# Differential-attention scores as one matmul per component instead of two, with a higher scheduling priority for the softmax chain

## The chip, the cores and the metric

The kernel runs on one core of one Trainium2 chip. The metric is the device time of one execution, in microseconds (us). Before the change it is 1974.8 us, the median of three runs (1973.25 to 1975.01). The engines are named as the profile names them: PE (TensorE, the matmul engine; PEld is its weight load), DVE (VectorE), ACT (ScalarE), POOL (GpSimd) and SP (the queue that issues the transfers). PEclk is the granted TensorE clock; 1.00 is 2.4 GHz.

## The reference, cut to what matters

Two decoder layers work on 512 tokens of 1024 features. Each layer is a feed-forward part, a mixer of four parallel groups, and a second feed-forward part. The change touches one group of the mixer, the differential attention: four heads of 64 features, each cut into two components of 32, causal, in four blocks of 128 queries.

```python
def _differential_attention(q, k, v, lam, lam_init, out_g):
    def one_block(args):
        qi, i = args
        s = jnp.einsum('bqhcd,bkhcd->bhcqk', qi, k).astype(jnp.float32) * scale
...
        p = jax.nn.softmax(jnp.where(causal, s, NEG_INF), axis=-1)
        a = p[:, :, 0] - lam * p[:, :, 1]
        return jnp.einsum('bhqk,bkhe->bqhe', a.astype(v.dtype), v)
```

So a head has two score matrices (c = 0 and 1), two softmaxes, and one product of their weighted difference with v. The queries and keys are RMS-normalised first.

## The kernel before

Every dense product is computed in a reduced-precision matmul type three times, to come close to float32: both factors are split into a high part and a low remainder, and `mm3` (L336 to L339) issues high by high, high by low and low by high. The weights are split on the chip, chunk by chunk in four pieces: ACT casts the high part (`wh`, L288) and DVE subtracts it (`wl`, L289). A ring of three buffers holds the raw chunks and their two halves.

The mixer projects its groups one after another: the convolution (`b`), queries and keys of the differential attention (`aqk`), its values (`av`), queries and keys of the second attention (`dqk`), its values and gates (`dvf`), the gating group (`c`), then the output projection (`wo`). When the columns of a group are there, a Python generator is started for its chain (`chain_a` for the differential attention), and every `mm3` call advances a clock by the matmul time that it stands for; when a chain's next step is due, its instructions are written between the matmuls of the projection that is running. So the attention runs in the shadow of `dqk`, `dvf` and `c`, and these matmuls are what PE does while a softmax is on DVE and ACT. The scheduler then orders each engine's queue by priority, which is the order of writing unless a block is wrapped in `tc.high_priority(offset=HX)`, which counts its instructions as written HX places earlier. Each engine works through its queue in order.

`attention_gen` (L1037) runs 16 units per layer, one for each head and query block, block fastest. Its step s multiplies the weights of unit s-2 with v (`weigh_v`, tile `poA`, then ACT scales into `oa`, L1035), computes scores and softmax of unit s (`stage1_a`, L1173), and transposes the weights of unit s-1 on PE (`ptA`, L1021) with a copy from PSUM by ACT (`pT`, L1026).

In `stage1_a` each component has a score tile `scA` of 128 queries by (i+1)*128 keys: two matmuls (high keys `aTh`, remainder of the keys `aTs`) and one matmul that adds the mask. `softmax` (L1004) takes the negated row maximum on DVE (`nmA`, L1007) and the exponential with its row sum on ACT (`p`, L1009). DVE then computes the reciprocal of both sums (`rA`, L1182), the factor `cf` (L1184) and the merged weights (`p`, L1185). The four blocks are 128, 256, 384 and 512 keys wide.

`prep_a` (L1200) makes the operands of one head, once for the queries (w = 0) and once for the keys (w = 1). The normalised columns `zr` hold each component twice (components 0, 0, 1, 1 in 32 columns each); PE transposes them to 128 rows (`aT`). For the queries ACT writes a scaled high part `aTh` (L1207) and, per component, a scaled copy masked by `gA` (`aTx`, L1212), and DVE combines the two with a `slot` pattern (`aTs`, L1214): in the 64 rows of the component lie the high part and the remainder, in the other 64 rows zeros. For the keys ACT writes the high part and DVE the remainder, both over all 128 rows (L1219). Head 0 is prepared at the start of the chain, each further head inside the units of the head before it (blocks 1 and 2).

Of the kernel before, what the change touches and what calls it, by code (L numbers as in the profile page):

```python
# [9 lines left out]
F32 = mybir.dt.float32  # L10
F32R = mybir.dt.float32r
BF16 = mybir.dt.bfloat16
I32 = mybir.dt.int32
AF = mybir.ActivationFunctionType
# [3 lines left out]
P = 128  # L18
# [6 lines left out]
def tile_hybrid_trunk(  # L25
# [47 lines left out]
    RSA, RSO, RSD, RSC, RSG = 0, 0, 0, 1, 1  # L73
    HX = 20
    Q = D // 4
# [16 lines left out]
    def blk(dt=F32, name="blk"):  # L92
        return bpool.tile([P, 512], dt, tag="blk", name=name)
# [68 lines left out]


    slot = const.tile([P, 2, 2], F32, name="slot")
    V.memset(slot, 0.0)
    for r in range(4):
        V.memset(slot[32 * r : 32 * r + 32, r // 2, 0:1], 1.0 - 2.0 * (r % 2))
        V.memset(slot[32 * r : 32 * r + 32, r // 2, 1:2], float(r % 2))
    fold = const.tile([P, P], F32, name="fold")
# [851 lines left out]
    def transpose_p(p, i, name):  # L1021
        pt = att(f"pt{name}")
        for j in range(i + 1):
            transpose(out=pt[:, j * P : (j + 1) * P], in_=p[:, j * P : (j + 1) * P], identity=ident)
        pT = blk(name="pT")
        A.copy(pT[:, : (i + 1) * P], pt[:, : (i + 1) * P])  # L1026
        return pT
# [43 lines left out]
    def mixer(l, hn, before, nxt):  # L1071
# [16 lines left out]
        V.tensor_scalar(ogs, cols[:, col_at["og"] + l : col_at["og"] + l + 1], 1.0 - lam_init, None, ALU.mult)  # L1088
        gA = small.tile([P, 4], F32, tag="gA", name=f"gA{l}")
        a0 = col_at["aq"] + 2 * l  # L1090
        V.tensor_scalar(gA[:, 0:1], cols[:, a0 : a0 + 1], 32 ** -0.5, None, ALU.mult)
        V.tensor_copy(gA[:, 1:2], cols[:, a0 + 1 : a0 + 2])
        V.tensor_scalar(gA[:, 2:4], slot[:, :, 1], gA[:, 0:1], None, ALU.mult)
        gD = small.tile([P, 2], F32, tag="gD", name=f"gD{l}")
# [78 lines left out]
        def stage1_a(i, hd):  # L1173
# [4 lines left out]
            for cc in range(2):  # L1178
                q, (kh, kl) = aT[hd][0][cc], aT[hd][1]
                sc = scores(((q, kh), (q, kl)), i, f"A{l}{i}{hd}{cc}", False)  # L1180
                pp.append(softmax(sc, n, s[:, cc : cc + 1], f"A{l}{i}{hd}{cc}"))
            V.reciprocal(r, s)  # L1182
            cf = small.tile([P, 1], F32, tag="cf", name=f"cf{l}{i}{hd}", bufs=4)
            V.scalar_tensor_tensor(cf, s[:, 0:1], nlam, r[:, 1:2], ALU.mult, ALU.mult)  # L1184
            V.scalar_tensor_tensor(pp[0][:, :n], pp[1][:, :n], cf, pp[0][:, :n], ALU.mult, ALU.add)  # L1185
            if hd < H - 1 and i in (1, 2):
# [13 lines left out]
        def prep_a(hd, w):  # L1200


            ps = att(f"aT{l}{hd}{w}")
            for t in range(NT):
                transpose(out=ps[:, t * P : (t + 1) * P], in_=zr[t, w][:, hd * P : (hd + 1) * P], identity=ident)
            hi = blk(F32R, "aTh")
            A.activation(hi, ps, AF.Identity, scale=gA[:, w : w + 1])  # L1207
            if w == 0:
                sts = []
                for cc in range(2):  # L1210
                    x_low = blk(name="aTx")
                    A.activation(x_low, ps, AF.Identity, scale=gA[:, 2 + cc : 3 + cc])  # L1212
                    st = blk(F32R, "aTs")
                    V.scalar_tensor_tensor(st, hi.bitcast(F32), slot[:, cc, 0:1], x_low, ALU.mult, ALU.add)  # L1214
                    sts.append(st)
                aT[hd] = [sts]
            else:
                st = blk(F32R, "aTs")
                V.scalar_tensor_tensor(st, ps, gA[:, 1:2], hi.bitcast(F32), ALU.mult, ALU.subtract)  # L1219
                aT[hd].append((hi, st))  # L1220

# [237 lines left out]
```

## Time and profile before

| | before |
|---|---|
| median of three runs | 1974.8 us |
| the profiled execution | 1977.86 us |
| its span in the trace | 1976.1 us (1.8 us lie around it) |
| PE busy | 1954.2 us, 99% |
| DVE busy | 1226.9 us, 62% |
| ACT busy | 725.1 us, 37% |
| granted TensorE clock, mean | 0.993 |

The busy shares are means over the whole span. The differential attention runs from about 454 us to 550 us in the first layer and about 970 us later in the second, so stretches of 10 us are read there. In a timeline a row is one instruction or a run of equal ones: start, time from the first start to the last end, engine, line, operation, output and inputs. Matmuls overlap, and the distance from one start to the next is what a matmul costs PE; the duration printed is longer. The bracket at a row's end is idle time of the engine just before it and the instruction that ended it.

### The profile page before, as it was taken

The numbers are of one execution on the slowest core, as the hardware profiler recorded it, in microseconds if no ns is written. First come the engines' busy times: TensorE is split into PE (matmuls) and PEld (weight loads), VectorE is DVE, ScalarE is ACT, GpSimd is POOL, SyncE is SP. The second block draws the span as 40 slices with busy tenths as digits, with TensorE's granted clock in tenths as the row PEclk, the third lists the DMA queues.
The fourth block names the chain that finished last, engine by engine and source line by source line (L and its number), as shares of the span: only waits on it lengthen the run. The fifth ranks groups of instructions, "written<-read, shape, count | busy, mean of one in ns | idle before, by whom it ended". The sixth has DMA issues, their size and how long they took to land.

```text
span 1976.1 us, 26140 instructions
## 1 busy us (share of the span) xinstructions
PE 1954.2 (99%) x10264; PEld 1661.3 (84%) x10264; DVE 1226.9 (62%) x2608; ACT 725.1 (37%) x1512; POOL 5.6 (0%) x18
## 2 busy tenths in 40 slices
PE   9999999999999999999999999999999999999999
PEld 7888888997889888888898888889887898888888
DVE  6776675588977776677575334337987773333332
ACT  4423222345764322323242222233366643222230
POOL 0000000000000000000000000000000000000000
PEclk8999999999999999999999999999999999999999
DMA  9665655221212566465433332322212122322311
GB/s 299 198 234 195 213 210 192 82 74 65 70 44 66 178 206 230 179 228 193 148 126 131 107 106 86 107 86 92 70 59 70 43 78 82 119 101 92 106 64 43
DMA packets 165350, 250.54 MB, mean 127 GB/s; under 512 B 6292, under 2 KB 112236, under 8 KB 165228
## 3 DMA queue, kind: packets, MB, share of 16 engines
q1 hardware_dynamic: 164640, 247.73, 37.2%
q8 instruction: 80, 1.31, 0.3%
q0 software_dynamic: 352, 1.05, 0.2%
q14 instruction: 42, 0.34, 0.1%
q10 hardware_dynamic: 236, 0.10, 0.0%
HBM read 246.76 MB, written 2.10 MB: 126 GB/s over the span
## 4 chain that ended last, share of the span: by engine, by line
PE 92%; DVE 5%; issue 1%; DMA 1%; ACT 1%; SPq 0%
PE i L337 15%; PE i L338 15%; PE i L339 15%; PE o L337 8%; PE o L338 8%; PE o L339 8%; PE wo L337 1%; DVE cacc L1130 1%; PE wo L339 1%; PE wo L338 1%; PE scA L143 1%; PE scD L143 1%; DVE wl L289 1%; PE poD L143 1%; PE dqk L337 1%
## 5 line engine op out<-in xcount | busy, mean ns | idle before, releaser
L289 DVE TENSOR_TENSOR wl<-w,wh 128x512 fp32r<-128x512 f32 (+3 forms) x652 | 401.2, 663 | 319.9 <-ACT wh L288 319.4
L288 ACT CAST wh<-w 128x512 fp32r<-128x512 f32 (+3 forms) x652 | 352.3, 600 | 666.1 <-issue 384.9
L337 PE MATMUL i<-hnh,wh 128*128 128x512 f32 (+1 forms) x1408 | 526.5, 376 | 2.2 <-ACT hnh L630 2.2
L338 PE MATMUL i<-hnl,wh 128*128 128x512 f32 (+1 forms) x1408 | 527.1, 375 | 0.3
L339 PE MATMUL i<-hnh,wl 128*128 128x512 f32 (+1 forms) x1408 | 526.4, 375 | 0.0
L337 PEld LDWEIGHTS i<-hnh,wh 128*128 128x128 f32 x1408 | 264.1, 188 | 49.4 <-ACT hnh L630 2.6
L338 PEld LDWEIGHTS i<-hnl,wh 128*128 128x128 f32 x1408 | 264.9, 188 | 48.0 <-DVE hnl L623 0.7
L339 PEld LDWEIGHTS i<-hnh,wl 128*128 128x128 f32 x1408 | 264.7, 188 | 47.8
L337 PE MATMUL o<-acth,wh 128*128 128x512 f32 (+1 forms) x832 | 297.9, 358 | 0.0
L338 PE MATMUL o<-actl,wh 128*128 128x512 f32 (+1 forms) x832 | 296.8, 357 | 0.0
L339 PE MATMUL o<-acth,wl 128*128 128x512 f32 (+1 forms) x832 | 296.6, 356 | 0.0
L337 PEld LDWEIGHTS o<-acth,wh 128*128 128x128 f32 x832 | 157.2, 189 | 22.6 <-DVE h L868 0.3
L339 PEld LDWEIGHTS o<-acth,wl 128*128 128x128 f32 x832 | 157.2, 189 | 22.6
L338 PEld LDWEIGHTS o<-actl,wh 128*128 128x128 f32 x832 | 157.2, 189 | 22.5
L501 DVE SCALAR_TENSOR_TENSOR acc<-ada,cond,acc 128x512 f32<-128x512 f32 x224 | 154.5, 744 | 24.2 <-DMA ada<-in_ada_w_dram 23.8
L937 DVE TENSOR_TENSOR silu<-silu,i 128x512 f32<-128x512 f32 x82 | 56.3, 687 | 158.5 <-PE i L339 158.5
L939 ACT CAST acth<-silu 128x512 fp32r<-128x512 f32 x88 | 54.4, 618 | 222.6 <-DVE silu L937 222.6
L868 DVE SCALAR_TENSOR_TENSOR h<-o,modc,h 128x512 f32<-128x512 f32 (+1 forms) x112 | 73.9, 671 | 70.6 <-PE o L339 70.0
L1130 DVE SCALAR_TENSOR_TENSOR cacc<-yp,cwc,cacc 128x512 f32<-128x512 f32 x120 | 89.5, 746 | 1.4
L941 DVE TENSOR_TENSOR actl<-silu,acth 128x512 fp32r<-128x512 f32 x88 | 60.5, 688 | 27.5 <-ACT acth L939 27.5
L630 ACT ACTIVATE hnh<-hn,modc 128x256 fp32r<-128x256 f32 x80 | 38.8, 506 | 72.3 <-DVE hn L629 72.3
L934 ACT ACTIVATE silu<-i 128x512 f32<-128x512 f32 x82 | 48.8, 596 | 31.9 <-PE i L339 31.9
(335 smaller groups left out, 2362.5 us busy)
## 6 DMA issues: line engine op xcount, KB each, us to landing
w<-in_ffn_w_in_dram SPq DMA_DIRECT2D x166, 512.0 KB
ada<-in_ada_w_dram SPq DMA_DIRECT2D x64, 1024.0 KB
w<-in_ffn_w_out_dram SPq DMA_DIRECT2D x40, 1024.0 KB
w<-in_w_in_dram SPq DMA_DIRECT2D x18, 1024.0 KB
w<-in_w_out_dram SPq DMA_DIRECT2D x8, 1024.0 KB
w<-in_ffn_w_in_dram SPq DMA_DIRECT2D x18, 256.0 KB
fpb<-in_ada_w_dram SPq DMA_DIRECT2D x16, 256.0 KB
w<-in_ffn_w_out_dram SPq DMA_DIRECT2D x8, 512.0 KB
```

The costliest lines, as they stand in the source:

```text
L143: return T.matmul(out, **kw)
L288: A.copy(wh[:, a], r[:, a])
L289: V.tensor_tensor(wl[:, a], r[:, a], wh[:, a].bitcast(F32), ALU.subtract)
L337: T.matmul(ps, lhsT=lh, rhs=rh, start=start, stop=False)
L338: T.matmul(ps, lhsT=lh, rhs=rl, start=False, stop=False)
L339: last_t[0] = T.matmul(ps, lhsT=ll, rhs=rh, start=False, stop=stop)
L501: last_v[0] = V.scalar_tensor_tensor(acc, src, cond[:, k : k + 1], acc, ALU.mult, ALU.add)
L868: V.scalar_tensor_tensor(h[m][:, a:b], ps[:, a:b], mcol(l, j, m), h[m][:, a:b], ALU.mult, ALU.add)
L937: last_v[0] = V.tensor_tensor(s, s, ps, ALU.mult)
L939: A.copy(ah, s)
L941: V.tensor_tensor(al, s, ah.bitcast(F32), ALU.subtract)
L1130: V.scalar_tensor_tensor(acc, ysl, w, acc, ALU.mult, ALU.add)
```

## The change

The keys get the same layout as the queries had in part: per component `st[cc]` holds 64 rows of the component's own high part and, in the other 64 rows, the remainder. The queries' `st[cc]` holds high part and remainder in the component's own 64 rows, and a copy of them in the other 64. One matmul over 128 rows then gives the sum that two matmuls gave. In `prep_a` the 128-row instructions of DVE become pairs over 64 rows, ACT's second `aTx` falls away, and two copies (queries) and one more activation (keys) of 64 rows come in. HX goes from 20 to 200, and the reciprocal, `cf`, the merge and the copy `pT` are put under it as well; the second attention shares `softmax` and `transpose_p`.

```diff
-    HX = 20
+    HX = 200
...
     def transpose_p(p, i, name):
...
         pT = blk(name="pT")
-        A.copy(pT[:, : (i + 1) * P], pt[:, : (i + 1) * P])
+        with tc.high_priority(offset=HX):
+            A.copy(pT[:, : (i + 1) * P], pt[:, : (i + 1) * P])
         return pT
...
             for cc in range(2):
-                q, (kh, kl) = aT[hd][0][cc], aT[hd][1]
-                sc = scores(((q, kh), (q, kl)), i, f"A{l}{i}{hd}{cc}", False)
+                sc = scores(((aT[hd][0][cc], aT[hd][1][cc]),), i, f"A{l}{i}{hd}{cc}", False)
                 pp.append(softmax(sc, n, s[:, cc : cc + 1], f"A{l}{i}{hd}{cc}"))
-            V.reciprocal(r, s)
             cf = small.tile([P, 1], F32, tag="cf", name=f"cf{l}{i}{hd}", bufs=4)
-            V.scalar_tensor_tensor(cf, s[:, 0:1], nlam, r[:, 1:2], ALU.mult, ALU.mult)
-            V.scalar_tensor_tensor(pp[0][:, :n], pp[1][:, :n], cf, pp[0][:, :n], ALU.mult, ALU.add)
+            with tc.high_priority(offset=HX):
+                V.reciprocal(r, s)
+                V.scalar_tensor_tensor(cf, s[:, 0:1], nlam, r[:, 1:2], ALU.mult, ALU.mult)
+                V.scalar_tensor_tensor(pp[0][:, :n], pp[1][:, :n], cf, pp[0][:, :n], ALU.mult, ALU.add)
...
-            hi = blk(F32R, "aTh")
-            A.activation(hi, ps, AF.Identity, scale=gA[:, w : w + 1])
+            own = (slice(0, 64), slice(64, 128))
+            st = [blk(F32R, "aTs") for _ in range(2)]
             if w == 0:
-                sts = []
+                hi = blk(F32R, "aTh")
+                A.activation(hi, ps, AF.Identity, scale=gA[:, 0:1])
+                x_low = blk(name="aTx")
+                A.activation(x_low, ps, AF.Identity, scale=gA[:, 2:3])
                 for cc in range(2):
-                    x_low = blk(name="aTx")
-                    A.activation(x_low, ps, AF.Identity, scale=gA[:, 2 + cc : 3 + cc])
-                    st = blk(F32R, "aTs")
-                    V.scalar_tensor_tensor(st, hi.bitcast(F32), slot[:, cc, 0:1], x_low, ALU.mult, ALU.add)
-                    sts.append(st)
-                aT[hd] = [sts]
+                    a, b = own[cc], own[1 - cc]
+                    V.scalar_tensor_tensor(st[cc][a], hi[a].bitcast(F32), slot[a, 0:1], x_low[a], ALU.mult, ALU.add)
+                    A.copy(st[cc][b], st[cc][a].bitcast(F32))
+                aT[hd] = [st]
             else:
-                st = blk(F32R, "aTs")
-                V.scalar_tensor_tensor(st, ps, gA[:, 1:2], hi.bitcast(F32), ALU.mult, ALU.subtract)
-                aT[hd].append((hi, st))
+                for cc in range(2):
+                    a, b = own[cc], own[1 - cc]
+                    A.activation(st[cc][a], ps[a], AF.Identity, scale=gA[a, 1:2])
+                    V.scalar_tensor_tensor(st[cc][b], ps[a], gA[a, 1:2], st[cc][a].bitcast(F32), ALU.mult, ALU.subtract)
+                aT[hd].append(st)
```

The queues of SP and POOL keep their order; those of PE, DVE and ACT change between the start of the differential attention and the first matmuls of the output projection. The places below are in the first layer, in the third head (head 2), from its third to its fourth block; the second layer has the same pattern.

PE before, from the second score tile of head 2, block 3 (512 keys): `ptA` x3 transposes the weights of block 2, `poA` x3 multiplies them with v, `dvf` is the projection that runs.

```order
L143 MATMUL scA_4584<-aTh,aTs 128x512
L143 MATMUL scA_4584<-aTs 128x512
L143 LDWEIGHTS identb
L143 MATMUL scA_4584<-maskb,identb 128x128
L339 MATMUL dvf_3_4396<-wh_4153,hnl 128x260
L337 MATMUL dvf_3_4396<-wh_4153,hnh 128x260
L338 MATMUL dvf_3_4396<-wl_4154,hnh 128x260
L339 MATMUL dvf_3_4396<-wh_4153,hnl 128x260
L147 MATMUL ptA_4596<-ident,p 128x128 x3
L337 MATMUL dvf_3_4396<-wh_4153,hnh 128x260
L338 MATMUL dvf_3_4396<-wl_4154,hnh 128x260
```

PE now, from the transposes of block 1 (`ptA` x2) on:

```order
L147 MATMUL ptA_4524<-ident,p 128x128 x2
L143 MATMUL poA_4555<-va,pT 128x64 x2
L143 MATMUL scA_4561<-aTs 128x512
L143 LDWEIGHTS identb
L143 MATMUL scA_4561<-maskb,identb 128x128
L143 MATMUL scA_4568<-aTs 128x512
L143 LDWEIGHTS identb
L143 MATMUL scA_4568<-maskb,identb 128x128
L147 MATMUL ptA_4579<-ident,p 128x128 x3
L143 MATMUL poA_4623<-va,pT 128x64 x3
L143 MATMUL scA_4630<-aTs 128x128
```

No projection matmul stands any more between `ptA` x2 and the transposes of block 3 (`ptA` x4). Before, 22 `dvf` matmuls stood between `ptA` x2 and `poA` x2, four between the scores of block 3 and `ptA` x3, and three between `ptA` x3 and `poA` x3; now all of them come earlier. Behind `ptA` x4 there were six matmuls of `c` ahead of `poA` x4, and now there are four.

ACT before, from the exponentials of block 2 (`p` of 384) to the copy `pT` of block 2, where `aTh` belongs to the preparation of head 3:

```order
L1009 ACTIVATE p,sA_4508<-scA_4510,nmA_4514 128x384
L1009 ACTIVATE p,sA_4508<-scA_4518,nmA_4522 128x384
L1207 ACTIVATE aTh<-aT_4530,gA_3265 128x512
L1026 COPY pT<-ptA_4539 128x256
L1035 ACTIVATE oa<-poA_4570,rA_4436 128x64
L1009 ACTIVATE p,sA_4574<-scA_4576,nmA_4580 128x512
L1009 ACTIVATE p,sA_4574<-scA_4584,nmA_4588 128x512
L1026 COPY pT<-ptA_4596 128x384
```

ACT now, the same stretch, with `wh` of the first chunk of `wo`:

```order
L286 CAST wh_4729<-w_4599 128x512
L1007 ACTIVATE p,sA_4493<-scA_4495,nmA_4498 128x384
L1007 ACTIVATE p,sA_4493<-scA_4502,nmA_4505 128x384
L1220 ACTIVATE aTs<-aT_4513,gA_3264 64x512
L286 CAST wh_4729<-w_4599 128x512 x3
L1220 ACTIVATE aTs<-aT_4513,gA_3264 64x512
L1025 COPY pT<-ptA_4524 128x256
L1034 ACTIVATE oa<-poA_4555,rA_4423 128x64
L1007 ACTIVATE p,sA_4559<-scA_4561,nmA_4564 128x512
L1007 ACTIVATE p,sA_4559<-scA_4568,nmA_4571 128x512
L1025 COPY pT<-ptA_4579 128x384
```

Between the second exponential of block 2 and the copy `pT` of block 1 stood one activation; now three casts and two activations stand there. In the queue before, these casts came behind the copy of block 2.

DVE before, from the row maxima of block 2 to those of block 3 (`dqk` is the normalisation for the second attention, `aTs` the preparation of head 3):

```order
L1007 TENSOR_REDUCE nmA_4522<-scA_4518 128x1
L1279 TENSOR_TENSOR dqk_4426<-zqk,ry_d_4413 128x8x64
L1279 TENSOR_TENSOR dqk_4480<-zqk,ry_d_4413 128x8x64
L1279 TENSOR_TENSOR dqk_4493<-zqk,ry_d_4413 128x8x64
L1182 RECIPROCAL rA_4509<-sA_4508 128x2
L1219 SCALAR_TENSOR_TENSOR aTs<-aT_4530,gA_3265,aTh 128x512
L1184 SCALAR_TENSOR_TENSOR cf_4527<-sA_4508,nlam_3260,rA_4509 128x1
L1279 TENSOR_TENSOR dqk_4544<-zqk,ry_d_4413 128x8x64
L1185 SCALAR_TENSOR_TENSOR p<-p,cf_4527 128x384
L1007 TENSOR_REDUCE nmA_4580<-scA_4576 128x1
```

DVE now, from the merge of block 2 to the row maxima of block 3:

```order
L1184 SCALAR_TENSOR_TENSOR p<-p,cf_4509 128x384
L190 TENSOR_TENSOR rt_d_4401<-ry_d_4400 128x32
L287 TENSOR_TENSOR wl_4590<-w_4394,wh_4589 128x512
L191 SCALAR_TENSOR_TENSOR rt_d_4401<-rt_d_4401,rv_d_4399 128x32
L1221 SCALAR_TENSOR_TENSOR aTs<-aT_4513,gA_3264,aTs 64x512
L192 SCALAR_TENSOR_TENSOR ry_d_4400<-rt_d_4401,ry_d_4400 128x32
L1129 SCALAR_TENSOR_TENSOR cacc<-yp_3566,cwc,cacc 128x512
L1005 TENSOR_REDUCE nmA_4564<-scA_4561 128x1
```

Between the merge of block 2 and the row maxima of block 3 nothing stood before; now a `wl`, the second `aTs` of head 3, a step of the convolution (`cacc`) and three short ones do. Ahead of that merge, behind its row maxima, stand now three `wl`, one `aTs` and six short ones instead of four `dqk`, one `aTs` and two short ones, and all four `dqk` stand between the row maxima and the merge of block 3, where three `wl` and one `cacc` stood.

## Rows read from the trace of the kernel before

**Rows 1.** The page, part 1: busy us, share of span, instructions.

```profile
PE 1954.2 (99%) x10264; PEld 1661.3 (84%) x10264; DVE 1226.9 (62%) x2608; ACT 725.1 (37%) x1512; POOL 5.6 (0%) x18
```

**Rows 2.** Stretches: PE, PEld, DVE, ACT, POOL busy, PEclk, DMA share, GB/s.

```profile
450.00:460.00 10.00, 6.73 (x30) 4.60 (x30) 10.00 (x24) 4.33 (x11) 0.00 (x0) 0.79 0.00 0
...
510.00:520.00 10.00, 8.43 (x62) 7.14 (x61) 10.00 (x25) 7.44 (x24) 0.75 (x1) 1.00 0.29 104
...
1480.00:1490.00 10.00, 8.43 (x62) 7.16 (x60) 10.00 (x25) 7.44 (x23) 0.75 (x1) 1.00 0.30 91
```

**Rows 3.** PE timeline: the second matmul of a score tile, 512 and 128 keys.

```profile
491.99 0.40 PE L143 MATMUL scA<-aTs 128*128 128x512 f32 x1
492.23 0.23 PE L143 MATMUL scA<-maskb,identb 128*128 128x128 bf16 x1
...
496.05 0.28 PE L143 MATMUL scA<-aTs 128*128 128x128 f32 x1
496.16 0.23 PE L143 MATMUL scA<-maskb,identb 128*128 128x128 bf16 x1
```

**Rows 4.** PE timeline: head 2, blocks 1 to 3 (transposes, products with v).

```profile
509.15 0.38 PE L147 MATMUL ptA<-ident,p 128*128 128x128 f32 x2
509.28 0.37 PE L338 MATMUL dvf<-wl,hnh 128*128 128x260 f32 x1
...
512.00 0.55 PE L143 MATMUL poA<-va,pT 128*128 128x64 f32 x4
...
515.84 0.88 PE L143 MATMUL poA<-va,pT 128*128 128x64 f32 x6 [0.89 <-ACT pT L1026]
...
518.00 0.63 PE L147 MATMUL ptA<-ident,p 128*128 128x128 f32 x4 [0.68 <-DVE p L1185]
518.39 0.49 PE L337 MATMUL c<-wh,hnh 128*128 128x512 f32 x1
...
519.87 1.09 PE L143 MATMUL poA<-va,pT 128*128 128x64 f32 x8
```

**Rows 5.** ACT, by line and form: an activation over 66 rows, all 16.

```profile
L1312 ACT ACTIVATE dT<-dT,gD x16: 665/681/690, 534.7 to 1512.1; 66x512 f32<-66x512 f32 x16
```

**Rows 6.** ACT timeline, head 2, blocks 1 to 3.

```profile
509.02 0.58 ACT L1009 ACTIVATE p<-scA,nmA 128x384 f32<-128x384 f32 x1 [0.25 <-DVE nmA L1007]
...
510.16 0.68 ACT L1207 ACTIVATE aTh<-aT,gA 128x512 fp32r<-128x512 f32 x1
510.73 0.37 ACT L1026 COPY pT<-ptA 128x256 f32<-128x256 f32 x1
...
513.97 0.69 ACT L1009 ACTIVATE p<-scA,nmA 128x512 f32<-128x512 f32 x1 [1.08 <-DVE nmA L1007]
...
516.97 1.65 ACT L288 CAST wh<-w 128x512 fp32r<-128x512 f32 x3
```

**Rows 7.** DVE timeline, head 2, blocks 2 and 3.

```profile
509.47 1.89 DVE L1279 TENSOR_TENSOR dqk<-zqk,ry_d 128x512 f32<-128x512 f32 x3
...
511.35 0.73 DVE L1219 SCALAR_TENSOR_TENSOR aTs<-aT,gA,aTh 128x512 fp32r<-128x512 f32 x1
...
512.73 0.61 DVE L1185 SCALAR_TENSOR_TENSOR p<-p,cf 128x384 f32<-128x384 f32 x1
513.25 1.28 DVE L1007 TENSOR_REDUCE nmA<-scA 128x1 f32<-128x512 f32 x2
514.45 1.29 DVE L289 TENSOR_TENSOR wl<-w,wh 128x512 fp32r<-128x512 f32 x2
...
516.45 0.74 DVE L1130 SCALAR_TENSOR_TENSOR cacc<-yp,cwc,cacc 128x512 f32<-128x512 f32 x1
```

**Rows 8.** PE timeline: the idle stretch of 452 us and the matmuls behind it.

```profile
454.20 0.33 PE L147 MATMUL aT<-ident,zr 128*128 128x128 f32 x1 [2.06 <-DVE zr L1227]
...
457.94 0.77 PE L337 MATMUL dqk<-wh,hnh 128*128 128x512 f32 x1
...
462.56 0.40 PE L338 MATMUL dqk<-wl,hnh 128*128 128x512 f32 x1
```

More of the change, by code (lines that the diff above doesn't have):

```diff
@@ L161, in tile_hybrid_trunk @@
     V.memset(onesc, 1.0 / 256.0)
-    slot = const.tile([P, 2, 2], F32, name="slot")
-    V.memset(slot, 0.0)
+    slot = const.tile([P, 2], F32, name="slot")
     for r in range(4):
-        V.memset(slot[32 * r : 32 * r + 32, r // 2, 0:1], 1.0 - 2.0 * (r % 2))
-        V.memset(slot[32 * r : 32 * r + 32, r // 2, 1:2], float(r % 2))
+        V.memset(slot[32 * r : 32 * r + 32, 0:1], 1.0 - 2.0 * (r % 2))
+        V.memset(slot[32 * r : 32 * r + 32, 1:2], float(r % 2))
     fold = const.tile([P, P], F32, name="fold")
@@ L1088, in mixer @@
         V.tensor_scalar(ogs, cols[:, col_at["og"] + l : col_at["og"] + l + 1], 1.0 - lam_init, None, ALU.mult)
-        gA = small.tile([P, 4], F32, tag="gA", name=f"gA{l}")
+        gA = small.tile([P, 3], F32, tag="gA", name=f"gA{l}")
         a0 = col_at["aq"] + 2 * l
@@ L1092, in mixer @@
         V.tensor_copy(gA[:, 1:2], cols[:, a0 + 1 : a0 + 2])
-        V.tensor_scalar(gA[:, 2:4], slot[:, :, 1], gA[:, 0:1], None, ALU.mult)
+        V.tensor_tensor(gA[:, 2:3], slot[:, 1:2], gA[:, 0:1], ALU.mult)
         gD = small.tile([P, 2], F32, tag="gD", name=f"gD{l}")
```

## The prediction, made before the changed kernel was run

> **What bounds the kernel now.** I read the page's busy shares first: PE is at work in 99% of the span, DVE in 62%, ACT in 37% [rows 1]. By the mean, a matmul that goes is time that goes. But the share is an average, and the change touches one stage, so I read the stretches of 10 us in it. From 510 to 520 us PE is busy 8.43 us of 10 and DVE all 10; the second layer has the same picture 970 us later, with 8.43 and 10.00 [rows 2]. In the PE timeline of that place the two gaps have names: 0.89 us ahead of `poA` for ACT's copy `pT`, and 0.68 us ahead of `ptA` for DVE's merge `p`, 1.57 us in all [rows 4]. So here the softmax chain across DVE, ACT and PE already sets the time, and PE hides it elsewhere only because projection matmuls stand between a score and its use: 22 of `dvf` run from 509.28 to 512.00, about 0.12 us each [rows 4]. The question is whether PE still has such cover, not how many matmuls go.
>
> **What PE saves.** The second matmul of a score tile costs its distance to the next start: 0.24 us at 512 keys and 0.11 at 128 [rows 3]. The widths between, 256 and 384, lie between these; on a line 0.15 and 0.20. There are 16 of each width over both layers, so 16 x 0.70 = 11.2 us, and 10.2 if the 256 wide one costs no more than 128. I take 10.6: 5.3 us per layer. This counts in full only while PE never waits.
>
> **What preparation adds.** Per head the queries need one activation less and two copies more on ACT, the keys one more; DVE has four instructions for three. All are over 64 rows instead of 128. ACT's activation over 66 rows took 681 ns, against 0.68 us for 128 [rows 5, 6], so half the rows are no cheaper there: ACT gets 2 x 0.6 = 1.2 us more per head, 4.8 per layer. For DVE the trace has no instruction of 64 rows and this width. By half the price of a full one (0.65 us, between the 0.63 of each of three `dqk` and the 0.73 printed for `aTs` [rows 7]) a head would cost 4 x 0.33 - 3 x 0.65 = 0.65 us less, by the full price 4 x 0.65 - 3 x 0.65 = 0.65 us more; ACT's row is the nearest, so I take the full price and keep a gain of 2.6 us per layer as the other bound, against a loss of 2.6. The Trainium skill (VectorE: DVE Perf Modes, "Why `tensor_reduce` can't reduce along partition axis") says that DVE streams along the free dimension and that its 128 lanes are independent, which is the full price too; no run here shows it for DVE. Changed `gA` and `slot` cost nothing: a few short instructions in the shadow of long projections. SP and POOL keep their order, so no transfer moves.
>
> **What the new order does to head 2.** Raising the chain by 200 places, with fewer score matmuls to write, shifts the projection: the 29 `dvf` matmuls that stood behind `ptA` x2 are now spent earlier. That is 29 x 0.12 = 3.5 us more PE work ahead of the scores of block 2, against 2 heads x 2 x 0.70 + 2 x (0.11 + 0.15) = 3.3 us of second matmuls saved by then. So PE reaches these scores about when it did, and the first exponential of block 2 starts near 509.4 (509.02 before [rows 6]). The saving of the first two heads has been turned into projection work done early, and behind it nothing covers the chain. I walk it from T = 509.4:
>
> ACT: two exponentials 1.14 (509.02 to 510.16), one `aTs` 0.57 (as `aTh`, 510.16 to 510.73), three casts 1.6, the other `aTs` 0.57, `pT` 0.37 [rows 6]. `poA` x2 starts at T + 4.3 = 513.7; it was 512.00 [rows 4]. PE finished `ptA` x2 at about T, so it idles some 4.3 us.
>
> DVE: the row maxima end at T + 0.45 (dqk started at 509.47 [rows 7]). Three `wl` at 0.62 (two span 1.29), one `aTs` 0.65, six short ones 0.6: the merge of block 2 starts at T + 3.5 and takes 0.52 (512.73 to 513.25). Then `wl` 0.62, `aTs` 0.65, `cacc` 0.66, three short ones 0.3: the row maxima of block 3 start at T + 6.3 [rows 7]. Their exponential follows 0.72 later (513.25 to 513.97), two take 1.35, `pT` 0.4 [rows 6, 7]: `poA` x3 at T + 8.8 = 518.2, before 515.84.
>
> Next, DVE needs 1.28 for these maxima, 4 x 0.63 for `dqk`, 0.2 for short ones and 0.65 for the merge: `ptA` x4 at T + 10.9 = 520.3, before 518.00. It takes 0.39, and four matmuls of `c` 4 x 0.25 (six took 518.39 to 519.87 [rows 4]): `poA` x4 at 521.7 instead of 519.87, 1.8 us late. Behind it PE has two more matmuls of `c` (+0.5) and saves those of head 3's wider blocks, 2 x 0.59 = 1.2: -0.7. The layer ends 1.1 us later. Counted the other way, 5.3 saved, the 1.57 of old gaps gone, and 4.3 + 3.1 + 1.0 of new idle (PE's own work between the three pauses is some 1.4 and 1.1 us): 1.5 later. Small hand-overs that I left out add to it. I take **+1.6 us per layer**, from +1.1 to +2.2.
>
> **The clock.** At 452 to 456 us PE idled 2.06 us ahead of `aT` and then ran only four short transposes with gaps. Behind it the granted clock was 0.79 over the slice [rows 2], and ten `dqk` matmuls and a transpose took from 457.94 to 462.56, over 0.42 us each instead of about 0.24, the 1.2 GHz level [rows 3, 8]. That cost half of 4.6 us, 2.3 us. The gaps of 0.89 and 0.68 us at 515 to 518 left the clock at 1.00 [rows 2, 4]. The new idle of 4.3 us is longer than either, so I expect the lower level behind it, and **2.3 us per layer** for it; nothing if the clock holds. The Trainium skill (TensorE: Matmul & The Clock Gate, "HAM oscillation — how this bites in real kernels") speaks against this change in the same sense: bursts of matmuls with long waits between them are throttled anew at each wait. By that rule all three pauses would be paid; by the rows the pauses cover most of the slow matmuls, and the sum has one.
>
> Sum: 2 x (1.6 + 2.3) = 7.8 us on the profiled execution's 1977.86, whose span is 1976.1. That execution is 3.1 us above the median of the runs, so the median goes from 1974.8 to about **1982.5**; the forecast's own range is 1979 to 1986.
>
> **The rivals.** (a) *The clock holds.* All as above, but PE does not fall to 1.2 GHz: 2 x 1.6 = 3.2, 1978.0, with 1973 to 1979 as its range if the DVE price or T is better by 1 to 2 us per layer. For it: the short gaps kept 1.00. Against: the 452 us stretch.
> (b) *PE keeps its saving* and the kernel gets faster. The mechanism is cover at the same place: if the chain of head 2 runs early enough that `pT` of block 1 is done by the time `ptA` x2 ends, and the merges of blocks 2 and 3 follow in PE's pace, the 5.3 us count and the old gaps go. That gives -10.6 to -13.7, 1961 to 1964; with one pause of 1 to 2 us left per layer 1965 to 1968. It decides at T: the first exponential would have to start some 4 us earlier than 509.4 relative to PE. For it: ACT is at 7.44 of 10 even in the tight stretch [rows 2], and 64-row instructions on DVE may be cheap. Against it: three casts and two activations now stand ahead of that copy in a queue, and five long DVE instructions ahead of two merges.
> (c) *The added preparation is on the path too.* In the stage DVE is full [rows 2]; if the three extra instructions at 0.65 delay T, another 2 us per layer: 1986.5.
> That the change fails to do what it says, by leaving score matmuls in, is excluded by the order.
>
> **How the numbers follow.** Forecast 0.47, (a) 0.25, (b) 0.20, (c) 0.08. About 0.2%, 4 us, is what a measurement of this kernel can tell from no change. Faster by more: (b), 0.20. Within: (a) and the low edge of the forecast, 0.28. Slower: the rest, 0.52. The range of 8 in 10 leaves out the better half of (b) and the end of (c): 1966 to 1988.
>
> **What would show it.** In the profile after: matmuls with scores `scA` once per tile; 29 `dvf` ahead of `ptA` x2 in head 2; PE waits there of 3 to 5 us on `pT` L1025 and 1 us on `p` L1184 in both layers; PE busy in the stretch 510 to 520 near 4 us; granted clock under 1.00 there. If PE's waits on `pT` total under 3 us over both layers, (b) holds and the order's lost cover was harmless; if they are long but the clock stays at 1.00, (a). If `scA` waits for `aTs`, (c). I would be wrong above all by T, which rests on DVE keeping its old pace through heads 0 and 1.

## The result, and the profile after

The changed kernel takes 1991.7 us (median of four runs, 1989.49 to 1992.17) against 1974.9 us (1973.25 to 1975.74) for the kernel before on the same chip: 16.8 us more, ratio 1.0084, 95% interval 1.0071 to 1.0096. The forecast was 7.6 us more, and the upper end of the range, 1988, lies 3.7 us below the measured time. The profiled execution took 1991.48 us, its span is 1989.7 us.

The page's line of busy times, to be set beside [rows 1]: 64 matmuls fewer, PE nevertheless busy longer, and ACT and DVE with 11.8 and 9.6 us more work.

```profile
PE 1956.8 (98%) x10200; PEld 1661.1 (83%) x10200; DVE 1236.5 (62%) x2615; ACT 736.9 (37%) x1528; POOL 5.6 (0%) x18
```

The stretches of [rows 2] again (length, PE, PEld, DVE, ACT, POOL, granted clock, DMA share, GB/s). The stage ran about 3 us earlier in the first layer, since the part before 450 us was 3 us shorter in this execution, and 7 us later in the second.

```profile
450.00:460.00 10.00, 7.42 (x19) 4.93 (x20) 8.57 (x18) 5.30 (x11) 0.00 (x0) 0.67 0.25 72
500.00:510.00 10.00, 8.59 (x69) 7.58 (x67) 9.24 (x26) 9.09 (x24) 0.00 (x0) 1.00 0.22 85
510.00:520.00 10.00, 5.32 (x22) 4.21 (x23) 9.81 (x24) 6.25 (x17) 0.76 (x1) 0.57 0.38 128
520.00:530.00 10.00, 10.00 (x39) 8.34 (x39) 6.10 (x19) 4.86 (x18) 0.00 (x0) 0.58 0.01 5
530.00:540.00 10.00, 9.22 (x48) 7.42 (x47) 7.19 (x23) 5.58 (x13) 0.00 (x0) 0.93 0.30 105
...
1490.00:1500.00 10.00, 5.18 (x21) 4.12 (x21) 9.82 (x24) 6.38 (x17) 0.75 (x1) 0.55 0.38 125
```

PE's busy time at 510 to 520 fell from 8.43 to 5.32, and then follow 10 us in which PE is busy throughout at a granted clock of 0.58: a busy PE that does little. The waits of PE (engine, line, waited for, us in total, times, longest) say for what:

```profile
PE poA L143 <- ACT pT L1025: 12.5, 8, 4.4
...
PE cum L143 <- DVE lf L1295: 1.6, 2, 0.8
```

And the PE timeline of head 2 shows where (the same place as [rows 4]; the bracket is idle time):

```profile
508.50 0.44 PE L147 MATMUL ptA<-ident,p 128*128 128x128 f32 x2
513.36 1.11 PE L143 MATMUL poA<-va,pT 128*128 128x64 f32 x4 [4.42 <-ACT pT L1025]
...
515.60 0.85 PE L147 MATMUL ptA<-ident,p 128*128 128x128 f32 x3
517.77 1.54 PE L143 MATMUL poA<-va,pT 128*128 128x64 f32 x6 [1.32 <-ACT pT L1025]
...
519.94 1.09 PE L147 MATMUL ptA<-ident,p 128*128 128x128 f32 x4
520.68 0.78 PE L335 MATMUL c<-wh,hnh 128*128 128x512 f32 x1
521.25 0.63 PE L336 MATMUL c<-wl,hnh 128*128 128x512 f32 x1
521.68 0.63 PE L337 MATMUL c<-wh,hnl 128*128 128x512 f32 x1
...
522.53 1.80 PE L143 MATMUL poA<-va,pT 128*128 128x64 f32 x8
```

ACT, between the exponentials of block 2 and the copy `pT` of block 1 (as [rows 6]):

```profile
508.86 0.58 ACT L1007 ACTIVATE p<-scA,nmA 128x384 f32<-128x384 f32 x1
...
509.98 0.68 ACT L1220 ACTIVATE aTs<-aT,gA 64x512 fp32r<-64x512 f32 x1
510.55 1.65 ACT L286 CAST wh<-w 128x512 fp32r<-128x512 f32 x3
512.23 0.68 ACT L1220 ACTIVATE aTs<-aT,gA 64x512 fp32r<-64x512 f32 x1
512.94 0.37 ACT L1025 COPY pT<-ptA 128x256 f32<-128x256 f32 x1
```

PE had its transposes (`ptA` x2) done by 508.9, and ACT came to their copy at 512.94, behind two halves of head 3's keys and three weight casts. From 521.25 on the `c` matmuls stand 0.43 us apart, the distance of the 1.2 GHz level in [rows 8].

To compare the layers apart from the varying start, I count from the first `aT` transpose of a layer: first layer to second 970.85 us before and 980.58 after (+9.7), second layer to the end 551.05 and 557.9 (+6.9).

### The profile page after: what moved, and what is told of

Its sections match the earlier page's. It is cut to its first block, busy times and chain, and to the rows that moved or that the text cites. A ratio compares the mean times of both kernels' runs of the same rounds, so it can differ in the third digit from the quotient of the medians.

```text
span 1989.7 us, 26027 instructions
## 1 busy us (share of the span) xinstructions
PE 1956.8 (98%) x10200; PEld 1661.1 (83%) x10200; DVE 1236.5 (62%) x2615; ACT 736.9 (37%) x1528; POOL 5.6 (0%) x18
## 4 chain that ended last, share of the span: by engine, by line
PE 91%; DVE 5%; ACT 2%; issue 1%; DMA 0%; SPq 0%; ACTq 0%; DVEq 0%
PE i L335 15%; PE i L336 15%; PE i L337 15%; PE o L335 8%; PE o L336 8%; PE o L337 8%; DVE cacc L1129 2%; PE wo L335 1%; PE wo L337 1%; PE wo L336 1%; PE poA L143 1%; PE scD L143 1%; PE ia L779 1%; PE poD L143 1%; DVE wl L287 1%
```

## The experiments

All ran beside the kernel before, whose medians were 1973.9 to 1975.1 us. Each ratio is to the kernel before on the same chip. What each left out of the computation stands in its expectation.

**Which half of the change?** e1_scores_only is the changed kernel with HX 20 and the chain outside the priority blocks; e2_prio_only is the kernel before with the new priority.

```diff
# e1_scores_only, against the changed kernel
-    HX = 200
+    HX = 20
...
-        with tc.high_priority(offset=HX):
-            A.copy(pT[:, : (i + 1) * P], pt[:, : (i + 1) * P])
+        A.copy(pT[:, : (i + 1) * P], pt[:, : (i + 1) * P])
...
# e2_prio_only, against the kernel before
-    HX = 20
+    HX = 200
...
-        A.copy(pT[:, : (i + 1) * P], pt[:, : (i + 1) * P])
+        with tc.high_priority(offset=HX):
+            A.copy(pT[:, : (i + 1) * P], pt[:, : (i + 1) * P])
...
```

> The product half alone: one matmul per score and the new preparation, with HX at 20 and the reciprocal, factor, merge and pT copy without raised priority. Theory P (the priority of 200 empties the cover of head 2, as the prediction put it): the cover comes back and about 10 us of matmuls are saved, 1964 to 1970. Theory S (the product half alone uses up the projection matmuls early; the priority does next to nothing): as the changed kernel, 1988 to 1993, with PE waiting some 4 us per layer for pT ahead of poA x2 of head 2, and the 1.2 GHz level behind it.

> The priority half alone: the kernel before with HX 200 and the reciprocal, factor, merge and pT copy raised. Theory P: slower than before by 5 us or more, waits on pT in head 2. Theory S: within 4 us of before, 1971 to 1978, no wait over 1.5 us in head 2 and the clock at 1.00 there.

Measured: e1 1990.54 us (ratio 1.0083, 1.0068 to 1.0098), with the same long pause:

```profile
PE poA L143 <- ACT pT L1024: 14.7, 8, 5.5
```

e2 1982.22 us (1.0040, 1.0025 to 1.0055). The product half alone (one matmul with its new preparation) makes the whole loss; the priority takes nothing from it and adds nothing. Beside the old preparation the priority costs some 8 us, so of e2's two theories P has the time and S the short waits: the longest wait on `pT` is 0.7 us. In its profiled execution (1979.55 us, the fastest of its four) the second layer has four waits of 0.42 to 0.68 us between 1484 and 1489 us and a granted clock of 0.92 and 0.91 over the 20 us there. The first layer has the same four waits, between 512 and 517 us, at a clock of 1.00. The second layer took 5 us more than before, the first 0.5 us. So the two halves don't add up: 8 beside the old preparation, nothing beside the new.

**Matmuls or preparation?** e3_twice issues the one score matmul twice; e8_twice_old_prio makes the same edit in e1_scores_only; e4_one_old_prep is the kernel before with one of its two score matmuls.

```diff
# e3_twice, against the changed kernel
-                sc = scores(((aT[hd][0][cc], aT[hd][1][cc]),), i, f"A{l}{i}{hd}{cc}", False)
+                sc = scores(((aT[hd][0][cc], aT[hd][1][cc]), (aT[hd][0][cc], aT[hd][1][cc])), i, f"A{l}{i}{hd}{cc}", False)
# e4_one_old_prep, against the kernel before
-                sc = scores(((q, kh), (q, kl)), i, f"A{l}{i}{hd}{cc}", False)
+                sc = scores(((q, kh),), i, f"A{l}{i}{hd}{cc}", False)
```

> The changed kernel with its one score matmul issued twice (the scores are doubled, so the output is another one): the new preparation with the old number of matmuls. If the added preparation on ACT and DVE is what costs (theory A), it is slower than the changed kernel by the 10.6 us of matmuls, about 2002. If the missing matmuls are what empties the cover (theory M), the waits shrink, 1976 to 1985. Both: waits of 2 to 3 us in head 2, 1988 to 1996.

> As e3 (new preparation, the score matmul issued twice, so the scores are doubled), with the old priorities. With e1, e3 and the changed kernel this gives the price of the matmuls and of the priority beside the new preparation. If the two halves add up, the priority costs what it cost the old preparation (8 us): 1991 to 1994. If the priority does next to nothing beside the new preparation (1 us, as between e1 and the changed kernel): 1998 to 2001.

> The kernel before with one score matmul per component (the product with the keys' remainder is left out, so the output is less exact) and the old preparation. Theory A: the whole saving arrives, about 1964. Theory M: PE waits ahead of poA x3 and ptA x4 of head 2 all the same, 1970 to 1985, and if the clock falls there the upper half of it.

Measured: e3 2000.58 us (1.0135, 1.0120 to 1.0150), e8 2000.67 (1.0126), e4 1972.7 (0.9990, 0.9980 to 0.9999, ten runs). With as many matmuls as before, the new preparation costs some 26 us (2000.58 against 1974.2). Beside it the missing matmuls are worth 8.9 us (with the priority) and 10.1 us (without), close to the 10.6 of the prediction. Beside the old preparation the same matmuls are worth 1.5 us (0.2 to 3.9 by the interval): there the longest wait on `pT` grows to 1.9 us, four such waits give 6.9 us in all. So the cover that the prediction feared for does matter: beside the old preparation its loss eats most of what the matmuls would give. But the 26 us are the preparation's.

**Which part of the preparation?** On DVE only the keys' single instruction became a pair; the queries had two before and have two now, over half the rows. All four runs are edits of e1_scores_only. e9_no_copies leaves ACT's two copies of the queries out and lets DVE write all 128 rows; e7_pool_copy puts the copies on POOL; e10_old_keys splits the keys as before, one activation and one DVE instruction over 128 rows; e11_keys_paired issues both activations of the keys ahead of their DVE instructions.

```diff
# e9_no_copies
-                    a, b = own[cc], own[1 - cc]
-                    V.scalar_tensor_tensor(st[cc][a], hi[a].bitcast(F32), slot[a, 0:1], x_low[a], ALU.mult, ALU.add)
-                    A.copy(st[cc][b], st[cc][a].bitcast(F32))
+                    V.scalar_tensor_tensor(st[cc], hi.bitcast(F32), slot[:, 0:1], x_low, ALU.mult, ALU.add)
# e10_old_keys
-                for cc in range(2):
-                    a, b = own[cc], own[1 - cc]
-                    A.activation(st[cc][a], ps[a], AF.Identity, scale=gA[a, 1:2])
-                    V.scalar_tensor_tensor(st[cc][b], ps[a], gA[a, 1:2], st[cc][a].bitcast(F32), ALU.mult, ALU.subtract)
+                A.activation(st[0], ps, AF.Identity, scale=gA[:, 1:2])
+                V.scalar_tensor_tensor(st[1], ps, gA[:, 1:2], st[0].bitcast(F32), ALU.mult, ALU.subtract)
# e7_pool_copy
-                    A.copy(st[cc][b], st[cc][a].bitcast(F32))
+                    nc.gpsimd.tensor_copy(st[cc][b], st[cc][a].bitcast(F32))
# e11_keys_paired
                 for cc in range(2):
-                    a, b = own[cc], own[1 - cc]
+                    a = own[cc]
                     A.activation(st[cc][a], ps[a], AF.Identity, scale=gA[a, 1:2])
+                for cc in range(2):
+                    a, b = own[cc], own[1 - cc]
                     V.scalar_tensor_tensor(st[cc][b], ps[a], gA[a, 1:2], st[cc][a].bitcast(F32), ALU.mult, ALU.subtract)
```

> As e1, but DVE writes all 128 rows of the queries' tiles and ACT's two copies per head fall away (the other 64 rows then hold the other component, so the scores are others). If the queries' copies are what the preparation costs (theory Q): as e4, 1972 to 1978. If it is the keys' split in two pairs of 64 rows (theory K): as e1, 1988 to 1992.

> The product half alone (as e1), with the two copies per head that fill the other 64 rows of the queries on POOL, not on ACT: ACT has 1.2 us less per head. If ACT's added work is what the preparation costs (theory A1), 1980 to 1986. If the cost is the order that follows from it, which this leaves as it was in head 2 (theory O), 1988 to 1992.

> As e1, but the keys are split as before, one activation and one DVE instruction over 128 rows (the high part serves component 0, the remainder component 1, so the scores are others); the queries keep their two copies on ACT. Theory Q: as e1, 1988 to 1992. Theory K: most of the 18 us between e1 and e4 come back, 1973 to 1980, and PE's longest wait for pT in head 2 falls from 5.5 us to under 3.

> As e1, with the keys' two activations written ahead of the two DVE instructions and not in turn; nothing else. If the alternation between ACT and DVE inside the keys' split is the cost: 1978 to 1985. If the number of instructions is, whatever their turn: 1988 to 1993.

| | us | ratio (95%) | wait of `poA` on `pT`: sum, longest |
|---|---|---|---|
| e1_scores_only | 1990.54 | 1.0083 (1.0068 to 1.0098) | 14.7, 5.5 |
| e9_no_copies | 1994.77 | 1.0105 (1.0090 to 1.0120) | 15.4, 5.7 |
| e7_pool_copy | 1994.64 | 1.0098 (1.0083 to 1.0114) | 18.1, 6.8 |
| e10_old_keys | 1973.96 | 0.9998 (0.9989 to 1.0008) | 7.4, 1.9 |
| e11_keys_paired | 1986.61 | 1.0062 (1.0045 to 1.0079) | 12.4, 3.4 |

The copies of the queries are not the cost: without them, or on POOL, it is some 4 us worse (2 to 3 us above the range that the theory left standing gave; why is not shown). So less work on ACT is not by itself less time here: each edit also brings another order. The keys' split into two pairs is the cost: with one pair, and the order that comes with it, 16.6 us go. By engine time it is little, one ACT and one DVE instruction per head, eight each in all, of 680 and 750 ns: 5.4 and 6.0 us, on engines that are busy 37% and 62% of the span (though DVE is full in the stage, [rows 2]). It shows in two places. The first is head 0, where PE writes the first scores. In the changed kernel ACT's two key activations (two copies of the queries stand between them), and the scores of the two components, stand apart (ACT, then PE):

```profile
456.42 0.68 ACT L1220 ACTIVATE aTs<-aT,gA 64x512 fp32r<-64x512 f32 x1 [1.75 <-PE aT L147]
...
458.67 0.68 ACT L1220 ACTIVATE aTs<-aT,gA 64x512 fp32r<-64x512 f32 x1 [0.16 <-DVE aTs L1221]
```

```profile
461.26 0.22 PE L143 MATMUL scA<-aTs 128*128 128x128 f32 x1
...
462.83 0.22 PE L143 MATMUL scA<-aTs 128*128 128x128 f32 x1
```

In e10_old_keys the same two scores follow each other:

```profile
460.93 0.22 PE L143 MATMUL scA<-aTs 128*128 128x128 f32 x1
...
461.36 0.22 PE L143 MATMUL scA<-aTs 128*128 128x128 f32 x1
```

PE does not idle between them, it runs `dqk` matmuls: 36 of them stand ahead of the first product with v, against 29 in e10 and 26 before. The chain is late from there on: from the first `aT` to the first exponential of head 2, block 2 it is 54.82 us before, 57.63 after, 57.80 in e1, 55.04 in e10. The filler is spent early: ahead of the first product of head 2 stand 67 `dvf` matmuls before, 96 after and in e1, 88 in e10. The second place is head 2. In e10 the copy `pT` of block 1 has one activation and two casts ahead of it instead of two and three, and starts at 509.21, 2.74 us behind that exponential (506.47); in the changed kernel it was 4.08 (508.86 to 512.94). And the eight `dvf` matmuls that are left stand between `ptA` x2 and the products of block 1, so that PE's wait there falls to 1.94 us (ACT, then PE):

```profile
507.61 0.68 ACT L1216 ACTIVATE aTs<-aT,gA 128x512 fp32r<-128x512 f32 x1
508.18 1.13 ACT L286 CAST wh<-w 128x512 fp32r<-128x512 f32 x2
509.21 0.38 ACT L1024 COPY pT<-ptA 128x256 f32<-128x256 f32 x1
```

```profile
506.37 0.38 PE L147 MATMUL ptA<-ident,p 128*128 128x128 f32 x2
506.50 0.37 PE L336 MATMUL dvf<-wl,hnh 128*128 128x260 f32 x1
...
509.64 0.66 PE L143 MATMUL poA<-va,pT 128*128 128x64 f32 x4 [1.94 <-ACT pT L1024]
```

What the missing matmuls save, e10 loses again in four waits of 7.4 us in all and a granted clock of 0.66 between 510 and 520 us, so it ends at the time of before.

e11_keys_paired takes away only the alternation, in which the second activation stands behind the first DVE instruction (in the changed kernel ACT's L1220 waited for L1221 four times, 3.0 us in all). In head 2 the activations then stand together, the casts fall behind the copy, and 4 of the 16.6 us go:

```profile
510.22 1.37 ACT L1218 ACTIVATE aTs<-aT,gA 64x512 fp32r<-64x512 f32 x2
511.61 0.37 ACT L1024 COPY pT<-ptA 128x256 f32<-128x256 f32 x1
512.01 0.62 ACT L286 CAST wh<-w 128x512 fp32r<-128x512 f32 x1
```

The time, 1986.61, lies between the ranges of its two theories, so neither holds alone. In head 0 a copy of the queries still stands between the two activations, the first score comes later than in e1, and the first exponential of head 2, block 2 is as late as it was (57.53 us from the first `aT`). So the 4 us come behind that point, and the late start is left as it was.

**The clock.** e5_after_dummy fills the pauses of blocks 1 and 2 in head 2 of the changed kernel with 36 matmuls each whose result nobody uses; e6_before_dummy puts such matmuls into the gaps at the first `aT` of the kernel before.

```diff
# e5_after_dummy, against the changed kernel
+        if name[0] == "A" and name[2:] in ("12", "22"):
+            for _ in range(36):
+                T.matmul(pt[:, (i + 1) * P :], lhsT=identb, rhs=wide[:, i + 1 :], start=True, stop=True)
# e6_before_dummy, against the kernel before
+                if hd == 0 and w == 0:
+                    for _ in range(2 if t else 9):
+                        T.matmul(ps[:, t * P : t * P + 64], lhsT=ident, rhs=rs_a[0], start=True, stop=True)
```

> The changed kernel with 36 dummy matmuls (256 wide, then 128 wide, bf16, into unread columns of the tile ptA) behind ptA x2 and behind ptA x3 of head 2, where PE waits for pT: about 3.9 and 2 us of PE work that nobody reads, and the order is otherwise the same. Theory C (the idle time brings the 1.2 GHz level, and that level costs 8.6 us in the first layer and 4.9 in the second by the profile): granted clock 1.00 through head 2, and 1977 to 1983. Theory W (the waits themselves are the loss, the clock under them costs little): 1989 to 1994.

> The kernel before with 15 dummy float32 matmuls, 64 wide, on the tile that the first transposes aT overwrite, as soon as the reciprocal roots of the differential attention are there: they fill the last 1.2 us ahead of aT of head 0 and the gaps between its transposes. If these idle 2.9 us are what lowers the clock until 462.6 us: clock 1.00 there and 3.1 us less per layer, 1967 to 1970. If the part of the wait that stays idle (1.1 us) or the time of the fall decides otherwise: 1973 to 1977.

Measured: e5 1989.76 us (ratio 1.0072, 1.0056 to 1.0087), 2 less than the changed kernel, though the intervals overlap; e6 1974.24 against 1975.06 for the kernel before (0.9996, 0.9986 to 1.0006), no difference that shows. Yet the clock did what was wanted. The stretches of e5_after_dummy:

```profile
510.00:520.00 10.00, 8.45 (x89) 7.21 (x86) 9.69 (x25) 6.82 (x19) 0.76 (x1) 1.00 0.38 116
520.00:530.00 10.00, 9.65 (x53) 7.81 (x52) 8.15 (x24) 8.14 (x25) 0.00 (x0) 1.00 0.07 23
530.00:540.00 10.00, 9.24 (x53) 7.37 (x52) 8.12 (x25) 3.93 (x10) 0.00 (x0) 0.83 0.26 98
```

The 0.57 and 0.58 became 1.00, and the pauses stayed, filled. The fourth block's products start 69.25 us behind the first `aT` instead of 71.30, so in the first layer the low clock of head 2 cost 2.05 us up to there and 4.3 us up to the last block of head 3 (91.49 instead of 95.82). In the second layer it cost 2.1 us up to the first products of head 3, of which 0.5 is left at its last block. Part of that went again behind the next waits (0.83 at 530 to 540), in the second layer all of it: from its first `aT` to the end 559.0 us against 557.9. So 14.7 of 16.8 us remain with the clock at full speed in both pauses. This is not yet a loss without any clock in it: the 0.83 is 3.4 us at the lower level, and e5 has two more stretches like it in the second layer (0.83 for 1510 to 1520, 0.89 for 1620 to 1635), where the kernel before has 1.00. By half of their length, an estimate from these rows, they could hold 5 us at most.

**Can the order be mended?** e12_prep_later moves the preparation of the next head in e11 from blocks 1 and 2 to blocks 2 and 3; e13_early_values also raises the copies that free the `dvf` tiles.

```diff
# e12_prep_later, against e11_keys_paired
-            if hd < H - 1 and i in (1, 2):
-                prep_a(hd + 1, i - 1)
+            if hd < H - 1 and i in (2, 3):
+                prep_a(hd + 1, i - 2)
# e13_early_values, against e12_prep_later
-            A.copy(pair_d[0][:, (t % 2) * 256 : (t % 2 + 1) * 256], ps[:, :256])
+            with tc.high_priority(offset=400):
+                A.copy(pair_d[0][:, (t % 2) * 256 : (t % 2 + 1) * 256], ps[:, :256])
+                V.tensor_tensor(fx[:, t * 4 : (t + 1) * 4], ps[:, 256:260], params["fb"][:, l, :], ALU.add)
...
-            V.tensor_tensor(fx[:, t * 4 : (t + 1) * 4], ps[:, 256:260], params["fb"][:, l, :], ALU.add)
```

> The changed kernel's product with the priority of before, the two activations of the keys written ahead of their two DVE instructions (as in e11_keys_paired), and the preparation of the next head moved from blocks 1 and 2 to blocks 2 and 3, so that in head 2 nine dvf matmuls stand again ahead of the transposes of block 1 and five ahead of the products of block 1. Nothing of the computation is left out. Theory C (what was lost is cover): with 14 matmuls (about 1.6 us) back at the place and the keys of head 3 out of the way of block 2, the longest wait on the copy pT falls under 2 us, their sum under 6 us, and the time to 1972 to 1980. Theory Q (the ACT queue): four casts still stand ahead of the copy pT of block 1, the longest wait stays 3 us or more, and the time stays at 1984 to 1988.

> As e12_prep_later, and the two copies that free the PSUM tiles of dvf are raised by 400 instructions, so that six matmuls of c (0.24 us each) can stand ahead of the transposes of block 3. Nothing of the computation is left out. Theory C: another 1.5 us of cover per layer, up to 3 us less than e12_prep_later, 1970 to 1978. Theory Q: the same time as e12_prep_later within 2 us, since the first pause stands ahead of these matmuls and the raised copies delay the softmax chain on ACT and DVE by as much.

Measured: e12 1987.02 us (1.0062, 1.0047 to 1.0077), e13 1993.5 (1.0093, 1.0076 to 1.0110). The theory of the ACT queue held for e12. ACT and PE of e12_prep_later:

```profile
504.99 0.69 ACT L1207 ACTIVATE aTh<-aT,gA 128x512 fp32r<-128x512 f32 x1
505.56 0.70 ACT L1209 ACTIVATE aTx<-aT,gA 128x512 f32<-128x512 f32 x1
506.12 2.19 ACT L286 CAST wh<-w 128x512 fp32r<-128x512 f32 x4
508.19 0.39 ACT L1024 COPY pT<-ptA 128x256 f32<-128x256 f32 x1
```

```profile
508.64 1.10 PE L143 MATMUL poA<-va,pT 128*128 128x64 f32 x4 [3.62 <-ACT pT L1024]
...
516.05 1.54 PE L143 MATMUL poA<-va,pT 128*128 128x64 f32 x6 [3.34 <-ACT pT L1024]
```

Five `dvf` matmuls stand again between `ptA` x2 and the products of block 1, but now the queries' activations and four casts stand ahead of the copy, and the pause is there again. The first exponential of head 2, block 2 is back at its old place here (54.55 us from the first `aT`, 54.82 before), although the second exponential of head 0 is 2.1 us late, as it is in e11; and the kernel still loses 12.5 us. So a late T is not the whole loss, and a late start of head 0 does not by itself make T late. e13 was 6.5 us worse still, where up to 2 was expected of this theory, so it bears out neither; its extra loss I did not follow. No version that computes everything beats the kernel before.

## Why the prediction was wrong

**The saving of PE: right.** 10.6 us forecast; e3 against the changed kernel gives 8.9, e8 against e1 10.1. Beside the old preparation (e4) only 1.5 of it arrives.

**Each instruction's price: right.** Half the rows cost what all cost. ACT's activation over 64 rows takes 680 ns (686 over 128 in e10), and DVE's took the full price that the prediction chose: in the changed kernel `aTs` (L1221) averages 750 ns over 64x512, and e10's takes 742 over 128x512. The gain of 2.6 us per layer at half the price was not there. The Trainium skill's statement that DVE streams along the free dimension and that its lanes are independent (VectorE: DVE Perf Modes, "Why `tensor_reduce` can't reduce along partition axis") agrees with these rows.

**Rival (c), the preparation on the path, was closer than its chance of 0.08 said.** The preparation does make T late, by about its price: 0.4 + 2 us a layer against 2.9 measured. That DVE's three added instructions do it is not shown, since e10 takes away ACT's activations with DVE's. Its time, 1986.5, was too low, and its sign, `scA` waiting for `aTs`, hardly appeared (0.3 us of a weight load): in the trace `dqk` matmuls fill that time.

**The terms, per layer.** Forecast beside measurement, mean of both layers, all counted from the first `aT`; T is the first exponential of head 2, block 2.

| | forecast, us | measured, us |
|---|---|---|
| T against before | +0.4 | +2.9 (2.8 and 3.1) |
| from T to the products of block 3 | +1.4 | +2.8 (2.8 and 2.8) |
| behind them, clock included | +2.1 | +2.5 (4.1 and 1.0) |
| sum | +3.9 | +8.3 |

The forecast's last row is its -0.7, +0.5 for hand-overs and 2.3 for the clock. The **step that failed is T**, 2.5 of the 4.4 us that are missing. The prediction said "PE reaches these scores about when it did", by 3.5 us of `dvf` moved ahead against 3.3 us of saved matmuls, and it began its walk at head 2. The trace of the first layer, from the first `aT` to the first product of head 2: `dvf` 67 to 96 matmuls, 3.9 us; scores -3.1; the same 96 `dqk` 0.6 longer; idle 0.9 more: 2.4 us later. So the two sizes were nearly right, each off to the same side, and idle time and slower `dqk` matmuls, which the balance had at nothing, are most of the rest. Its last sentence named this weak place: T "rests on DVE keeping its old pace through heads 0 and 1". The chain did not keep it. The lag is there at the first product of head 0 (2.1 us in the first layer and 2.4 in the second, ahead of the first `dvf`), and the exponentials are 3.7 us late at the last block of head 0 and 4.3 at that of head 1.

With e10's single pair of keys T is 0.2 us later than before, near the 0.4 of the forecast, so the keys' split makes T late. By which of its steps is not shown: e11 and e12 leave the start of head 0 late, and T is late in e11 and not in e12.

**The chain from T: right by its steps.** Pauses of 4.42 and 1.32 us stand where the prediction put them, in both layers. It had 4.3, 3.1 and 1.0. The second is shorter and the third is missing because PE's own work between them ran at the lower clock: 3.1 and 2.2 us (513.36 to the second pause, 517.77 to 519.94) instead of 1.4 and 1.1. So part of the slow clock lies in time that would have been idle, as the prediction said. Forecast and measured distances from T: `poA` x2 (block 1) 4.3 and 4.5, `poA` x3 8.8 and 8.9, `ptA` x4 10.9 and 11.1, `poA` x4 12.3 and 13.7. The last is the clock, since four `c` matmuls took 1.85 us instead of the 1.0 of the sum; in e5, at full clock, it is about 12. PE was busy 5.32 us between 510 and 520, forecast near 4, for the same reason.

**Its cause: wrong in its first half.** The prediction put the lost cover down to "Raising the chain by 200 places, with fewer score matmuls to write". e1 has the old priority and the same loss, and e8 against e3 shows no effect of it. The fewer matmuls do cost cover (e4), but no time beside the kernel before. The loss needs the preparation's instructions: e10 gives back the time with the keys' instructions alone.

**The clock: the mechanism came, and the size is open.** At 510 to 520 us it stood at 0.57, and at 0.55 in the second layer. The prediction had 2.3 us per layer; e5 shows 4.3 and 2.1 up to the first products of head 3, and by the runs 2 for both layers together. The prediction took the length from one stretch of 4.6 us. In the trace PE ran at the low level from 513.4 to 528.3 us, 10 us past the last pause, and in the first layer it came again behind the 0.78 us wait of `cum` (granted clock 0.59 from 538 to 542); the second layer has the same wait at a clock of 1.00. The rule of the Trainium skill that bursts with long waits between them are throttled anew at each wait (TensorE: Matmul & The Clock Gate, "HAM oscillation — how this bites in real kernels") agrees with the pause of 4.42 us, in both layers; for the short waits no rule comes out of these rows. Since e5, which holds the clock through both pauses, gains only 2 us by the runs, the clock in the pauses alone doesn't explain the miss.

Open remain: how the keys' split makes T late; e2's 8 us beside the old preparation, of which I saw only the short waits and, in one layer, the clock behind them; why e7 and e9 are slower than e1; e13's 6.5; and the tie that makes ACT's second activation wait for DVE's first instruction, which e11 removes without showing its reason.

## What to carry to other kernels

Price a step that other engines must run before a matmul by the place where its result is first needed, not by the busy shares of the engines: two instructions of 0.7 us per head, on engines that were busy 37% and 62% of the span, cost more than 64 matmuls gave. Where a change splits an instruction over fewer rows, look for the alternation between engines that comes with it, and issue each engine's pieces together; here that gave back 4 of 16.6 us. And walk the chain from the first unit that the change touches, and count the filler as you go: what the order puts into a gap in head 0 hides the wait there, and is missing in head 2.

## What the runs showed of the hardware

Instructions over 64 rows cost as much as over 128: on DVE 750 ns (changed kernel) and 742 (e10), on ACT 680 and 686, for 512 columns. A copy of 64x512 takes 782 ns on POOL (e7) and 619 on ACT. The low clock outlasted its cause: PE ran at 1.2 GHz until 528.3, though its last pause had ended at 517.8. Like waits did not always bring it: e2 has the same four waits of 0.42 to 0.68 us in both layers, with a granted clock of 1.00 in the first and 0.92 in the second. And a clock brought back to full speed gave little back: e5 kept 1.00 through head 2 and gained 2 us; e6 had 1.00 from 450 to 460 us (0.79 before) and gained nothing that the runs can tell.
